# Moving the weight tiles and the x tiles of a decoder layer by 32 and 64 bytes in SBUF

## The chip, the cores and the metric

The kernel runs on one core of a Trainium2 chip. The metric is the device time of one execution in microseconds (us), as the median of several runs. The matrix engine, TensorE (PE in the profile), multiplies a stationary operand of 128x128, which a weight load (PEld) puts in place, by a moving operand of up to 512 columns. VectorE (DVE), ScalarE (ACT) and GpSimd (POOL) do the elementwise work. The queue of SyncE (SP) issues nearly all transfers from HBM. [...]

## The reference

One decoder layer on x of 512 tokens by 1024 channels, in float32: a half-step SwiGLU feed-forward block (FFN), a mixer in which a recurrent group of channels and 8 heads of stick-breaking attention stand side by side, and a second half-step FFN. Cut to what matters here:

```python
def _swiglu(x, w_gate, w_up, w_down):
    return (jax.nn.silu(x @ w_gate) * (x @ w_up)) @ w_down

x = x + 0.5 * _swiglu(_rms_norm(x, ffn1_norm), ffn1_w_gate, ffn1_w_up, ffn1_w_down)
h = _rms_norm(x, mix_norm)
xr, gate, q, k, v = split(h @ w_in)
y_rnn = _rg_lru_group(xr, gate, ...)
y_att = _stick_breaking(norm(q), norm(k), v)
x = x + concat(norm(y_rnn), norm(y_att)) @ w_out
x = x + 0.5 * _swiglu(_rms_norm(x, ffn2_norm), ffn2_w_gate, ffn2_w_up, ffn2_w_down)
```

The FFN's inner width is 2816. Nearly all of the work is the products of x with the weights.

## The kernel before

x is held transposed, channels across the 128 partitions, as eight tiles of 128x512. Each float32 operand is split into a high and a low part of the type float32r, and a product is three matmuls: high by high, high by low, low by high (`mm3`, L142 to L145). So a weight tile `r_...` that a transfer brings becomes a tile `h_...` (a cast on ACT, L133) and a tile `l_...` (a subtraction on DVE, L135), and x becomes `xh_...` and `xl_...` (L157, L159).

The work in order of time:

- The first stage (L529 to L580): 16 small matmuls on constants, then the products for the first three blocks of the first FFN. Their weights have tiles of their own, `first_r`, `first_h` and `first_l`, in a pool of their own. For each of x's eight tiles and each of the three kinds of product, six matmuls follow each other, one per weight tile, into six PSUM banks.
- The rest of the first FFN: plain products for three more blocks (L143 to L145), then sixteen blocks in pairs by a scheme that adds and subtracts halves of the matrices to save products (`fast`, L397, with moving operands of 256 columns, or 512 in some steps). Between its steps lie blocks of the down projection (L143 to L145), whose moving operands are `hh` and `hl`.
- The mixer: projections with w_in (L143 to L145; for q, k and v the weights are the moving operand and x's parts the stationary one), small gates, scores, transposes through `ident`, and w_out.
- The second FFN, as the first (tiles ending in b instead of a), without a stage of its own pool.

The order of each engine's instructions is fixed when the program is built, by a scheduler; at run time an instruction waits only for its operands and for room. The places of the tiles in SBUF are fixed then too: the pools lie one behind the other, and each tile takes the next free address, its size rounded up to 32 bytes per partition. The pool `const` comes first (`mhalf`, `warm`, `ones`, `ident`, `fut`, ...), then `wpool` (all `r_`, `h_`, `l_` tiles of weights), then `xpool` (`x0`, in which the vectors of gains and biases stand behind x's first 512 columns, x1 to x7, `xh`, `xl`), then `stat`, then the pools of the stages (`first`, then `ffn_a`, ...). A change in the size of an early tile thus moves all that lie behind it.

Of the kernel before, what the change touches and what calls it, by code (L numbers as in the profile page):

```python
# [8 lines left out]
F32 = mybir.dt.float32  # L9
# [6 lines left out]
P = 128  # L16
# [30 lines left out]
C_G1, C_GM, C_G2 = 0, 8, 16  # L47
C_CW, C_CB, C_BA, C_BX, C_LAM = 24, 40, 44, 48, 52
C_RN, C_AN, C_QN, C_KN = 56, 60, 64, 65
NVEC = 66  # L50


@with_exitstack
def hybrid_layer_kernel(
# [17 lines left out]
    const = ctx.enter_context(tc.tile_pool(name="const", bufs=1))  # L72
# [22 lines left out]

    mhalf = const.tile([P, 8], F32, tag="mhalf", name="mhalf")
    nc.vector.memset(mhalf, -0.5)
    warm = const.tile([P, 8], F32, tag="warm", name="warm")
    nc.scalar.activation(warm, mhalf, AF.Sigmoid)
    ones = const.tile([P, P], F32, tag="ones", name="ones")  # L100
# [19 lines left out]

    x0 = xpool.tile([P, T + NVEC], F32, tag="x0", name="x0")
    vec = x0[:, T:]
# [409 lines left out]
    def first_products():  # L532

        with tc.tile_pool(name="first", bufs=1, reuse_waits="tile") as fi:
# [8 lines left out]
            for kk in range(KD // 2):  # L543
                s = slice(2 * kk * P, (2 * kk + 2) * P)
                c = 2 * kk * T + NVEC
                if kk == 0:
                    nc.sync.dma_start(x0, xT[:, : T + NVEC])
                else:
# [562 lines left out]
def _layout(x, ffn1_norm, ffn1_w_gate, ffn1_w_up, ffn1_w_down, mix_norm, w_in,  # L1111
            conv_w, conv_b, rg_w_a, rg_b_a, rg_w_x, rg_b_x, rg_lambda,
            q_norm, k_norm, rnn_out_norm, attn_out_norm, w_out,
            ffn2_norm, ffn2_w_gate, ffn2_w_up, ffn2_w_down):
    import numpy as np

    def cols(v):
        return np.asarray(v).reshape(-1, P).T

    def by_block(w):  # L1120

        k, n = w.shape
        return w.reshape(k // P, P, n // P, P).transpose(2, 1, 0, 3).reshape(n // P, P, k)

    def by_pairs(w):


        o = by_block(w).reshape(NF, P, KD, P)
        o = np.concatenate([o[:, :, 0::2], o[:, :, 1::2]], axis=2).reshape(NF, P, KD * P)
        o = np.concatenate([o[1::2], o[0::2]], axis=2)  # L1130
        b = by_block(w)
        o[: PLAIN // 2] = np.concatenate([b[0:PLAIN:2], b[1:PLAIN:2]], axis=2)
        return o

    w = np.asarray(w_in)[0]
    qkv = w[:, 2 * DR :].reshape(KD // 2, 2, P, 3, DR).transpose(3, 0, 2, 1, 4)
    def gates(a, x):

        a, x = np.asarray(a)[0], np.asarray(x)[0]
        o = np.empty((P, NJ, P), a.dtype)  # L1140
        for n in range(2 * NJ):
            r = (n % 2) * HD
            o[r : r + HD, n // 2, r : r + HD] = a[n]
            o[r : r + HD, n // 2, HD - r : 2 * HD - r] = x[n]
        return o.reshape(P, NJ * P)

    def swapped(v):

        return np.asarray(v).reshape(-1, 2, HD)[:, ::-1].reshape(-1)

    vecs = np.concatenate(
        [
            cols(ffn1_norm[0]), cols(mix_norm[0]), cols(ffn2_norm[0]), cols(conv_w[0]),
            cols(conv_b[0]), cols(rg_b_a[0]), cols(swapped(rg_b_x[0])), cols(rg_lambda[0]),
            cols(rnn_out_norm[0]), cols(attn_out_norm[0]),
            cols(np.tile(np.asarray(q_norm[0]), 2)), cols(np.tile(np.asarray(k_norm[0]), 2)),
        ],
        axis=1,
    )

    xt = np.asarray(x)[0].T.reshape(KD, P, T).transpose(1, 0, 2).reshape(P, KD * T)
    a = {
        "xT": np.concatenate([xt[:, :T], vecs, xt[:, T:]], axis=1),
        "w_rg": by_block(w[:, : 2 * DR]),
        "w_qkv": qkv.reshape(3, KD // 2, P, 2 * DR),
        "w_gate": gates(rg_w_a, rg_w_x),
        "w_out": by_block(np.asarray(w_out)[0]),
        "wg1": by_pairs(np.asarray(ffn1_w_gate)[0]),
        "wu1": by_pairs(np.asarray(ffn1_w_up)[0]),
        "wd1": by_block(np.asarray(ffn1_w_down)[0]),  # L1170
        "wg2": by_pairs(np.asarray(ffn2_w_gate)[0]),
        "wu2": by_pairs(np.asarray(ffn2_w_up)[0]),
        "wd2": by_block(np.asarray(ffn2_w_down)[0]),
    }
    return {n: np.ascontiguousarray(a[n]) for n in _INS}
# [21 lines left out]
```

## Time and profile before

| | |
|---|---|
| median of 3 runs | 909.22 us (908.8 to 909.35) |
| the profiled execution | 908.92 us |
| its span, first to last instruction | 907.1 us |
| PE busy | 901.0 us, 99% of the span, 4880 matmuls |
| weight loads busy | 758.1 us, 84% |
| DVE busy | 712.9 us, 79% |
| ACT busy | 466.9 us, 51% |
| POOL busy | 72.9 us, 8% |
| moved by DMA | 89.18 MB, 29.0% of the 16 engines' time on the main queue |

The duration that the profile gives for a matmul (about 395 ns for 512 columns) includes the way through the array, and the next one starts before it is over; what a stream of matmuls costs is read from the distance between starts, here called the spacing. PE's busy share therefore also covers short gaps.

### The profile page before, as it was taken

The numbers are of one execution on the slowest core, as the hardware profiler recorded it, in microseconds if no ns is written. First come the engines' busy times: TensorE is split into PE (matmuls) and PEld (weight loads), VectorE is DVE, ScalarE is ACT, GpSimd is POOL, SyncE is SP. The second block draws the span as 40 slices with busy tenths as digits, with TensorE's granted clock in tenths as the row PEclk, the third lists the DMA queues.
The fourth block names the chain that finished last, engine by engine and source line by source line (L and its number), as shares of the span: only waits on it lengthen the run. The fifth ranks groups of instructions, "written<-read, shape, count | busy, mean of one in ns | idle before, by whom it ended". The sixth has DMA issues, their size and how long they took to land.

```text
span 907.1 us, 12596 instructions
## 1 busy us (share of the span) xinstructions
PE 901.0 (99%) x4880; PEld 758.1 (84%) x4880; DVE 712.9 (79%) x1032; ACT 466.9 (51%) x771; POOL 72.9 (8%) x60
## 2 busy tenths in 40 slices
PE   9999999999999999999999999999999999999998
PEld 7888899888988888877887678888899888998887
DVE  8598789887887669758689959697689967896763
ACT  7254365544653446365768844445256534563450
POOL 0000000000000005544140001400000000000000
PEclk9999999999999999999999999999999999999999
DMA  8323322331232222322132002324322332233202
GB/s 284 106 62 138 115 93 93 133 141 53 94 128 93 76 93 83 115 72 103 58 116 71 25 24 94 117 66 149 117 93 93 120 129 78 93 112 99 88 24 92
DMA packets 27452, 89.18 MB, mean 98 GB/s; under 512 B 2817, under 2 KB 6145, under 8 KB 23297
## 3 DMA queue, kind: packets, MB, share of 16 engines
q1 hardware_dynamic: 27248, 88.26, 29.0%
q8 instruction: 38, 0.62, 0.3%
q14 instruction: 22, 0.17, 0.1%
q10 hardware_dynamic: 144, 0.13, 0.0%
HBM read 86.28 MB, written 2.10 MB: 97 GB/s over the span
## 4 chain that ended last, share of the span: by engine, by line
PE 98%; DVE 1%; DMA 0%; issue 0%; ACT 0%; DVEq 0%
PE pxua L397 5%; PE pxub L397 5%; PE pxgb L397 5%; PE pxga L397 5%; PE pdb L144 5%; PE pdb L145 5%; PE pdb L143 5%; PE pda L144 5%; PE pda L145 5%; PE pda L143 5%; PE pyua L397 4%; PE pyga L397 4%; PE pygb L397 4%; PE pyub L397 4%; PE first_p L580 4%; PE po L143 2%
## 5 line engine op out<-in xcount | busy, mean ns | idle before, releaser
L144 PE MATMUL pdb<-hlb,h_db 128*128 128x512 f32 (+2 forms) x180 | 70.1, 391 | 0.0
L145 PE MATMUL pdb<-hhb,l_db 128*128 128x512 f32 (+2 forms) x180 | 69.7, 391 | 0.0
L143 PE MATMUL pdb<-hhb,h_db 128*128 128x512 f32 (+2 forms) x180 | 69.3, 391 | 0.0
L144 PE MATMUL pda<-hla,h_da 128*128 128x512 f32 x176 | 69.2, 395 | 0.0
L145 PE MATMUL pda<-hha,l_da 128*128 128x512 f32 x176 | 68.9, 395 | 0.0
L143 PE MATMUL pda<-hha,h_da 128*128 128x512 f32 x176 | 68.0, 395 | 0.0
L482 DVE SCALAR_TENSOR_TENSOR x<-pdb,x 128x512 f32<-128x512 f32 (+2 forms) x33 | 21.9, 673 | 35.8 <-PE pdb L145 35.8
L133 ACT CAST h_da<-r_da 128x768 fp32r<-128x768 f32 (+1 forms) x28 | 24.2, 867 | 43.5 <-PE pda L144 21.4
L133 ACT CAST h_db<-r_db 128x768 fp32r<-128x768 f32 (+1 forms) x28 | 24.2, 868 | 41.3 <-PE pdb L144 21.8
L482 DVE SCALAR_TENSOR_TENSOR x<-pda,x 128x512 f32<-128x512 f32 x32 | 21.6, 687 | 27.2 <-PE pda L145 27.2
L145 PEld LDWEIGHTS pdb<-hhb,l_db 128*128 128x128 f32 x180 | 33.8, 188 | 7.7
L144 PEld LDWEIGHTS pdb<-hlb,h_db 128*128 128x128 f32 x180 | 33.8, 188 | 7.2
L143 PEld LDWEIGHTS pdb<-hhb,h_db 128*128 128x128 f32 x180 | 33.8, 188 | 6.9
L145 PEld LDWEIGHTS pda<-hha,l_da 128*128 128x128 f32 x176 | 33.0, 187 | 7.9
L144 PEld LDWEIGHTS pda<-hla,h_da 128*128 128x128 f32 x176 | 33.0, 187 | 7.3
L143 PEld LDWEIGHTS pda<-hha,h_da 128*128 128x128 f32 x176 | 33.0, 188 | 7.1
L173 POOL TENSOR_TENSOR sqa_m<-sqa_m,sq_m 128x512 f32<-128x512 f32 x7 | 11.8, 1681 | 312.4 <-ACT sq_m L172 312.2
L377 ACT CAST h_gb<-rgb 128x512 fp32r<-128x512 f32 (+1 forms) x24 | 18.4, 765 | 24.2 <-PE pdb L144 12.8
L135 DVE TENSOR_TENSOR l_da<-r_da,h_da 128x768 fp32r<-128x768 f32 (+1 forms) x28 | 27.7, 989 | 2.9 <-ACT h_da L133 2.9
L135 DVE TENSOR_TENSOR l_db<-r_db,h_db 128x768 fp32r<-128x768 f32 (+1 forms) x28 | 27.7, 992 | 2.9 <-ACT h_db L133 2.9
L377 ACT CAST h_ua<-rua 128x512 fp32r<-128x512 f32 (+1 forms) x24 | 18.3, 764 | 22.5 <-PE pyga L397 8.8
L377 ACT CAST h_ub<-rub 128x512 fp32r<-128x512 f32 (+1 forms) x24 | 18.4, 765 | 22.1 <-PE pygb L397 8.8
(459 smaller groups left out, 2821.3 us busy)
## 6 DMA issues: line engine op xcount, KB each, us to landing
r_da<-in_wd SPq DMA_DIRECT2D x24, 384.0 KB, 3.1
r_db<-in_wd SPq DMA_DIRECT2D x24, 384.0 KB, 3.1
rga<-in_wg SPq DMA_DIRECT2D x8, 1024.0 KB, 5.7
rua<-in_wu SPq DMA_DIRECT2D x8, 1024.0 KB, 4.7
rgb<-in_wg SPq DMA_DIRECT2D x8, 1024.0 KB, 5.0
rub<-in_wu SPq DMA_DIRECT2D x8, 1024.0 KB, 4.8
r_o<-in_w_out SPq DMA_DIRECT2D x8, 512.0 KB, 3.5
r_gb<-in_wg SPq DMA_DIRECT2D x6, 512.0 KB, 3.8
```

The lines of the kernel that those rows point to most:

```text
L133: nc.scalar.copy(hi, raw)
L135: nc.vector.tensor_sub(lo, raw, f32(hi))
L143: nc.tensor.matmul(out_, wh, ah, start=start, stop=False)
L144: nc.tensor.matmul(out_, wh, al, start=False, stop=False)
L145: return nc.tensor.matmul(out_, wl, ah, start=False, stop=stop)
L173: (engine or nc.gpsimd).tensor_add(self.acc, self.acc, sq)
L377: nc.scalar.copy(hi[:, to], a)
L397: nc.tensor.matmul(pt[:, : r.shape[1]], l[:, s], r, start=start and (k, i) == order[0], stop=(k, i) == order[-1], skip_group_check=True,)
L482: nc.vector.scalar_tensor_tensor(x[k][:, t], pt[:, t], 0.5, x[k][:, t], op0=ALU.mult, op1=ALU.add)
L580: nc.tensor.matmul(pts[i], wp[i][:, s], xp[k], start=k == 0 and wp is hi and xp is n1.h, stop=k == KD - 1 and wp is lo,)
```

## The change

The change adds a tile of eight float32 columns, which nothing reads or writes, between `mhalf` and `warm` in the pool `const`, and 14 columns of zeros behind the vectors in `x0` (NVEC goes from 66 to 80; the host's array gets the same zeros).

```diff
-NVEC = 66
+NVEC = 80
...
     nc.vector.memset(mhalf, -0.5)
+    const.tile([P, 8], F32, tag="space", name="space")
     warm = const.tile([P, 8], F32, tag="warm", name="warm")
...
             cols(np.tile(np.asarray(q_norm[0]), 2)), cols(np.tile(np.asarray(k_norm[0]), 2)),
+            np.zeros((P, NVEC - C_KN - 1), np.float32),
```

What it does to the places in the built program, as the remainder of a tile's start address on division by 64, and by 128 in brackets (x0's row with vectors grows from 2312 to 2368 bytes, and the room that it takes from 2336 to 2368):

| tiles | before | after | moved by |
|---|---|---|---|
| `ones`, `ident`, `fut` and the other constants behind `warm` | 0 (64) | 32 (96) | 32 |
| weights in `wpool`: `r_`, `h_`, `l_` | 0 (64) | 32 (96) | 32 |
| `x0` | 0 (64) | 32 (96) | 32 |
| x1 to x7, `xh`, `xl` | 32 (96) | 32 (32) | 64 |
| weights of the first stage: `first_r`, `first_h`, `first_l` | 32 (96) | 32 (32) | 64 |
| FFN tiles: `hh`, `hl`, `xb`, `g`, `o`, `raw`, `sums` | 32 (96) | 32 (32) | 64 |
| mixer: `qT`, `kT`, `gate_h`, `gate_l` | 32 (96) | 32 (32) | 64 |
| mixer: `xch`, `xcl` | 0 (0) | 0 (64) | 64 |

Slices of weights start at multiples of 512 bytes inside their tile, and the moving operands of 512 columns at multiples of 2048.

No instruction is added or removed. The transfer of x0 brings 592 instead of 578 columns. The orders of DVE, ACT, POOL and SP are the same but for the numbers of the tiles. On PE one matmul of the first stage moves back. Before, the product of the last low weight tile (`first_l_138`) with x's first tile (`xh_a_172`) comes ahead of the products with x's second tile (`xh_a_188`):

```order
L580 MATMUL first_p_127<-xh_a_172,first_l_126 128x512
L580 MATMUL first_p_135<-xh_a_172,first_l_134 128x512
L580 MATMUL first_p_139<-xh_a_172,first_l_138 128x512
L580 MATMUL first_p_119<-xh_a_188,first_h_117 128x512
L580 MATMUL first_p_123<-xh_a_188,first_h_121 128x512
L580 MATMUL first_p_127<-xh_a_188,first_h_125 128x512
L580 MATMUL first_p_131<-xh_a_188,first_h_129 128x512
L580 MATMUL first_p_135<-xh_a_188,first_h_133 128x512
L580 MATMUL first_p_139<-xh_a_188,first_h_137 128x512
```

Now, with every line and tile number one higher, it stands five places later in the same stretch of PE's order:

```order
L581 MATMUL first_p_128<-xh_a_173,first_l_127 128x512
L581 MATMUL first_p_136<-xh_a_173,first_l_135 128x512
L581 MATMUL first_p_120<-xh_a_189,first_h_118 128x512
L581 MATMUL first_p_124<-xh_a_189,first_h_122 128x512
L581 MATMUL first_p_128<-xh_a_189,first_h_126 128x512
L581 MATMUL first_p_132<-xh_a_189,first_h_130 128x512
L581 MATMUL first_p_136<-xh_a_189,first_h_134 128x512
L581 MATMUL first_p_140<-xh_a_173,first_l_139 128x512
L581 MATMUL first_p_140<-xh_a_189,first_h_138 128x512
```

Only this matmul moved; the rest of PE's 4393 rows keeps its order.

## Rows read from the trace of the kernel before

**Rows 1.** The page: busy time of the engines (us, share of the span, instructions), and the chain that ended last, by engine.

```profile
PE 901.0 (99%) x4880; PEld 758.1 (84%) x4880; DVE 712.9 (79%) x1032; ACT 466.9 (51%) x771; POOL 72.9 (8%) x60
...
PE 98%; DVE 1%; DMA 0%; issue 0%; ACT 0%; DVEq 0%
```

**Rows 2.** The view of waits, PE alone: who waited for whom, us in total, times, the longest. These are all its rows.

```profile
PE warm L529 <- DVE ones L101: 1.1, 1, 1.1
PE py L1012 <- DVE yal L1027: 0.8, 1, 0.8
PE pw L993 <- DVE be L984: 0.6, 1, 0.6
PE first_p L580 <- ACT xh_a L157: 0.5, 1, 0.5
PE py L1012 <- ACT wt L1004: 0.3, 1, 0.3
```

**Rows 3.** The chain that ended last, from 105 to 114 us, in order of time: start in us, us on the chain, what. On the chain a matmul's us is its spacing.

```profile
105.13 0.23 PE pda L143
...
107.23 1.40 PE pxga L397 x8
108.64 1.40 PE pyga L397 x8
110.04 1.41 PE pxua L397 x12
111.45 1.41 PE pyua L397 x12
```

**Rows 4.** The timeline of PE in the first stage: start in us, us, what, and how many matmuls the row merges.

```profile
8.57 0.39 PE L580 MATMUL first_p<-xh_a,first_h 128*128 128x512 f32 x1
8.80 0.39 PE L580 MATMUL first_p<-xl_a,first_h 128*128 128x512 f32 x1
9.02 1.07 PE L580 MATMUL first_p<-xh_a,first_l 128*128 128x512 f32 x4
9.93 0.39 PE L580 MATMUL first_p<-xh_a,first_h 128*128 128x512 f32 x1
...
14.01 1.52 PE L580 MATMUL first_p<-xh_a,first_h 128*128 128x512 f32 x6
15.37 1.52 PE L580 MATMUL first_p<-xl_a,first_h 128*128 128x512 f32 x6
...
20.81 0.39 PE L580 MATMUL first_p<-xh_a,first_l 128*128 128x512 f32 x1
...
35.22 1.65 PE L580 MATMUL first_p<-xh_a,first_h 128*128 128x512 f32 x6
36.70 1.54 PE L580 MATMUL first_p<-xl_a,first_h 128*128 128x512 f32 x6
38.08 1.52 PE L580 MATMUL first_p<-xh_a,first_l 128*128 128x512 f32 x6
39.44 0.60 PE L200 MATMUL psr_a<-ident,r_a 128*128 128x128 f32 x4
```

**Rows 5.** Busy time by stretch: the stretch in us and its length; then busy us and instructions of PE, PEld, DVE, ACT, POOL; granted share of PE's full clock, DMA share, GB/s.

```profile
15.00:20.00 5.00, 5.00 (x24) 4.14 (x23) 5.00 (x12) 5.00 (x14) 0.00 (x0) 1.00 0.96 312
35.20:37.60 2.40, 2.40 (x12) 1.98 (x12) 0.16 (x1) 0.00 (x0) 1.02 (x1) 1.00 0.00 1
39.40:60.00 20.60, 20.60 (x92) 16.61 (x91) 20.60 (x34) 11.06 (x16) 0.00 (x0) 1.00 0.13 39
100.00:150.00 50.00, 50.00 (x335) 45.66 (x335) 41.15 (x61) 27.61 (x48) 0.00 (x0) 1.00 0.26 91
625.00:645.00 20.00, 20.00 (x88) 16.05 (x87) 17.89 (x32) 6.40 (x12) 0.00 (x0) 1.00 0.68 244
```

**Rows 6.** The same kind of view for the stretch behind the first stage, once each for the matmuls of L143, L144, L145 and L397: PE busy and its instructions, PEld busy and its instructions.

```profile
39.50:907.10 867.60, 284.92 (x724) 135.85 (x724) 1.00 0.28 93
...
39.50:907.10 867.60, 284.74 (x724) 135.86 (x724) 1.00 0.28 93
...
39.50:907.10 867.60, 283.97 (x724) 135.78 (x724) 1.00 0.28 93
...
39.50:907.10 867.60, 322.42 (x2128) 294.35 (x2128) 1.00 0.28 93
```

**Rows 7.** Groups of PE's instructions by line and shape: count, busy us, mean ns of one. Here the weights are the moving operand and a part of x the stationary one.

```profile
L144 PE MATMUL pk<-l_k,xh_m 128*128 128x512 f32 x32 | 12.7, 395 | 0.0
```

**Rows 8.** Groups of ACT's and DVE's instructions by line and shape, as in rows 7.

```profile
L377 ACT CAST h_ga<-rga 128x512 fp32r<-128x512 f32 x16 | 10.0, 622 | 9.5 <-PE pda L144 9.0 <-PE pyga L397 0.3
L271 ACT CAST hha<-gga 128x512 fp32r<-128x512 f32 x16 | 9.6, 620 | 3.8 <-DVE gga L457 1.8 <-DVE gga L456 1.4 <-PE pda L145 0.7
L378 DVE TENSOR_TENSOR l_ga<-rga,h_ga 128x512 fp32r<-128x512 f32 x16 | 10.9, 683 | 0.1
L272 DVE TENSOR_TENSOR hla<-gga,hha 128x512 fp32r<-128x512 f32 x16 | 10.5, 685 | 0.3 <-ACT hha L271 0.2
```

**Rows 9.** The timeline around 176 us, where a pair's high part becomes ready on ACT and PE takes it.

```profile
176.18 0.61 ACT L271 CAST hha<-gga 128x512 fp32r<-128x512 f32 x1
...
176.85 0.39 PE L143 MATMUL pda<-hha,h_da 128*128 128x512 f32 x1
```

## The prediction

> **What bounds the kernel now.** I read the engines' busy times and the chain first. PE is busy for 901.0 of 907.1 us, and the chain that ended last is 98% PE [rows 1]. PE's waits come to 3.3 us in all [rows 2]. So the time is the number of matmuls times their spacing, and a change that moves no work can only act on the spacing. That is what I read next, in two places.
>
> Behind the first stage the spacing of a 512-column matmul is 233 ns: from 105.13 to 107.23 us lie nine matmuls of the down projection, 2.10/9 = 233.3 ns [rows 3]. A 256-column matmul takes half of that: eight of `pxga`, four of either width, take 1.40 us, as 4 x 233.3 + 4 x 116.7 does, and twelve narrow ones take 1.40 to 1.41 us [rows 3].
>
> In the first stage it is shorter. From 14.01 to 20.81 us lie 30 matmuls of 512 columns: 6.80/30 = 226.7 ns [rows 4]. The granted clock is 1.00, the 2.4 GHz level, in both [rows 5], so the clock doesn't part them: 226.7 ns are 544 of its cycles, 32 more than there are columns, and 233.3 ns are 560, 48 more.
>
> **What differs between the two.** Not the load: from 15 to 20 us DVE and ACT are busy all the time and the DMA engines 96% of it, and the spacing is the short one [rows 4, 5]. Not the six matmuls in a row with one moving operand either: from 8.57 to 9.93 us it is xh, xl, then xh with low weights, and six matmuls take 1.36 us, 226.7 ns [rows 4]. What is left is the place of the operands. In the first stage weights and x's parts both stand at 32 modulo 64. Behind it one stands at 0 and the other at 32: weights at 0 and the moving x, `hh` or `xb` at 32, or, for q, k and v, moving weights at 0 and stationary x at 32; the matmul then lasts 395 ns like the others of the long spacing [rows 7].
>
> The short spacing is not there from the start. After the small matmuls on `sqa` at 35 us the next six take 36.70 - 35.22 = 1.48 us, of which the first takes some 0.32, so 232 ns each for five; the next six 1.38 us, 230 ns; the last six 39.44 - 38.08 = 1.36 us, 226.7 ns [rows 4]. No transfer runs then and DVE and ACT are next to idle [rows 5]. With equal places PE falls into the short spacing after some ten matmuls; with unequal places it never does.
>
> **The change part by part.**
>
> The weights go from 0 to 32 modulo 64, and x's parts and the FFN's tiles stay at 32. So all large products stand as the first stage does, modulo 64. I take the spacing to become 226.7 and 113.3 ns. Counts: L143 to L145 have 3 x 724 = 2172 matmuls, of which 24 belong to the last split block and are narrower (12 of 384, 12 of 128 columns), leaving 2148 of 512. L397 has 2128 [rows 6]. By the code an FFN has eight pairs with a g and a u matrix each; ten of these sixteen matrices (all g, and u of pairs 6 and 9) run their seven products with four matmuls of 512 and four of 256 columns, so 2 x 10 x 28 = 560 matmuls of L397 have 512 columns and 1568 have 256. Gain: (2148 + 560) x 6.6 ns = 17.9 us, and 1568 x 3.3 ns = 5.2 us: 23.1 us together.
>
> What comes off it. Each break in the stream (a transpose, a gate, an idle moment) costs the fall into the short spacing: 5 x 5.3 + 6 x 3.3 = 46 ns by the rows at 35 us [rows 4]. The mixer has some 60 such breaks (42 steps of the attention's order and some 18 gates and turns), so 2.8 us at most; many breaks are closer together than ten matmuls and then nothing is gained between them either, which the same figure covers. I take 1.5 us.
>
> PE is also fed just in time at some places. The pair at 176 us has its high part ready at 176.79 and PE takes it at 176.85 [rows 9]. If PE's fill work between a pair's last product and this point, some 8 us, shrinks by 2.8%, PE waits up to 0.23 us there. There are 16 such pairs: at most 3.7 us, and I take 2.0. From 39.4 us on DVE has no idle time for 20.6 us [rows 5], but there is no wait of PE there, and DVE is back at 82% by 100 to 150 us (41.15 of 50), 85% after a gain of 2.8%. It stays off the path.
>
> The rest costs nothing. ACT's casts take 622 ns into weights at 0 and 620 ns into `hh` at 32, DVE's subtractions 683 and 685 ns [rows 8], so the engines that write the moved tiles don't care. Transfers into weights at 32 ran at 312 GB/s with a DMA share of 0.96 in the first stage, and into weights at 0 at 244 with 0.68 [rows 5]: 325 against 359 GB/s of busy time, so a moved transfer takes 0 to 10% longer; PE waits for none of them [rows 2]. The 14 columns are 7 KB more in the first transfer, 0.02 us at 312 GB/s, ahead of the first product. The one matmul that moved in the first stage keeps the stage's work as it was, at most one spacing of 0.2 us either way.
>
> Sum: 23.1 - 1.5 - 2.0 = 19.6 us. The profiled execution took 908.9 us, so 889.3; the median of the runs is 0.3 us higher: **889.6 us**.
>
> A rule that speaks against this: the Trainium skill, "SBUF — State Buffer", section "Door 1: The DMA port swizzle", gives SBUF lines of 16 bytes, and 32 bytes are two whole lines, so by it a shift of 32 changes nothing. "TensorE: Matmul & The Clock Gate", section "Step-by-step: what each phase is for", says that loading the next weights takes no read bandwidth from the running matmul, so their relative place shouldn't count; by these rules the time stays at 909.2 us. The two spacings of 226.7 and 233.3 ns in one trace don't agree with them, unless something else parts the stages.
>
> **The rivals.**
>
> *The place isn't the cause* (chance 0.14): the first stage has six PSUM banks in turn and six weight tiles far apart, and I can't exclude that these give the short spacing; the stretch at 8.57 us, with its changing operands, speaks against it but is short. Then nothing moves: 909.2 us, 908.4 to 910.0.
>
> *Only the plain products gain* (0.14): in L397 two widths alternate every four matmuls, fewer than the ten that the fall into the short spacing took, and the trace has no 256-column matmul with equal places. Then 2148 x 6.6 ns = 14.2 us less the same 1.5 and 2.0: 10.7 us, 898.5 us.
>
> *Slower* (0.10): in the first stage weights and x's parts are equal modulo 128 too (96 and 96); after the change the large products have weights at 96 and x's parts at 32. If what counts repeats every 128 bytes and the price grows with the distance, the rows give 226.7 ns at distance 0 and 233.3 at 32, and one more such step makes 239.9 at 64: 23.1 us lost in place of 23.1 won, 932.0 us. It decides as soon as the down projection's spacing passes 233.3. For it: no row of before has the distance 64. Against it: the short spacing has 32 cycles more than columns, one for each 16 columns or 64 bytes of a moving row, which makes 64 the natural length, and by that the two places are equal.
>
> **How the numbers follow.** Forecast 0.62, the others 0.14, 0.14 and 0.10. The forecast's own range is 885 (no deduction, 886.1, less a little) to 895 us. The range that holds 8 in 10 takes in the partial gain and no change and leaves out the slower case: 885 to 910 us. Faster by over 0.2% (1.8 us, about what a measurement of this kernel can tell from none): 0.62 + 0.14 = 0.76; the same 0.14; slower 0.10.
>
> **What would show it.** Right: the nine matmuls that now span 2.10 us span 2.04, the narrow twelve 1.36 instead of 1.40, and single matmuls last 0.39 us throughout, as in the first stage [rows 4]. The first stage keeps 6.80 us for 30. Wrong in the cause: the spacing stays at 233.3. Wrong in size: the plain products at 226.7 and those of L397 at 233.3, or PE's waits grow beyond the 3.3 us of now by more than 2.0. The prediction as a whole is wrong if the spacing of the down projection doesn't fall.

## The result, and the profile after

The changed kernel takes 898.77 us in the median (898.72 to 898.83, four runs), the kernel before, measured beside it, 909.04 us (908.8 to 909.35). The ratio is 0.9888, with a 95% interval of 0.9872 to 0.9903: 10.3 us faster. The profiled execution took 898.83 us, and its span is 897.0.

The page of the changed kernel: busy times, and the chain by engine.

```profile
PE 891.2 (99%) x4880; PEld 758.0 (84%) x4880; DVE 712.1 (79%) x1032; ACT 466.2 (52%) x771; POOL 72.9 (8%) x60
...
PE 98%; DVE 1%; DMA 1%; issue 0%; ACT 0%; SPq 0%; DVEq 0%
```

PE's waits in the changed kernel: who waited for whom, us in total, times, the longest. These are all its rows.

```profile
PE warm L530 <- DVE ones L102: 1.1, 1, 1.1
PE py L1013 <- DVE yal L1028: 0.8, 1, 0.8
PE pw L994 <- DVE be L985: 0.7, 1, 0.7
PE py L1013 <- ACT wt L1005: 0.3, 1, 0.3
PE first_p L581 <- ACT first_h L565: 0.2, 1, 0.2
```

PE still bounds the kernel, with the same 98% of the chain, and its waits come to 3.1 us for 3.3 [rows 1, 2]. So the gain lies in the spacing, and the chain has it. From the changed kernel's chain, start in us, us on the chain, what:

```profile
103.11 0.23 PE pda L146
...
105.17 0.23 PE pda L146
...
106.08 1.37 PE pxga L398 x8
107.45 1.38 PE pyga L398 x8
108.84 1.41 PE pxua L398 x12
110.25 1.41 PE pyua L398 x12
```

Nine matmuls of the down projection lie between 103.11 and 105.17 us: 2.06/9 = 228.9 ns, for 233.3 before [rows 3]. The eight of `pxga` take 1.37 us for 1.40. The twelve narrow ones take 1.41 us, no less than the 1.40 to 1.41 of before. The timeline shows how 228.9 comes about:

```profile
104.78 0.39 PE L145 MATMUL pda<-hla,h_da 128*128 128x512 f32 x1
105.00 0.39 PE L146 MATMUL pda<-hha,l_da 128*128 128x512 f32 x1
105.23 0.39 PE L144 MATMUL pda<-hha,h_da 128*128 128x512 f32 x1
105.47 0.39 PE L145 MATMUL pda<-hla,h_da 128*128 128x512 f32 x1
105.69 0.39 PE L146 MATMUL pda<-hha,l_da 128*128 128x512 f32 x1
105.92 0.62 PE L398 MATMUL pxga<-xb_sa,h_ga 128*128 128x512 f32 x2
...
106.84 0.39 PE L398 MATMUL pxga<-xb_sa,l_ga 128*128 128x256 f32 x2
107.06 0.39 PE L398 MATMUL pxga<-xh_sa,l_ga 128*128 128x256 f32 x2
107.29 0.62 PE L398 MATMUL pyga<-xb_sa,h_ga 128*128 128x512 f32 x2
```

The starts repeat in threes: 0.24, 0.22, 0.23 us, in the trace's nanoseconds 232, 226 and 229. It is a third spacing, between the two of the kernel before. Behind the wide matmuls the four narrow ones from 106.84 to 107.29 take 0.45 us, 113 ns each, but in the long narrow runs the spacing is 1.41/12 = 117.5 ns. The first stage in the changed kernel, its weights and x's parts both moved by 64 bytes, keeps its 30 matmuls from 14.11 to 20.91 us, 6.80/30 = 226.7 ns, as in [rows 4]:

```profile
14.11 1.52 PE L581 MATMUL first_p<-xh_a,first_h 128*128 128x512 f32 x6
15.47 1.52 PE L581 MATMUL first_p<-xl_a,first_h 128*128 128x512 f32 x6
...
20.91 0.39 PE L581 MATMUL first_p<-xh_a,first_l 128*128 128x512 f32 x1
```

The groups of the changed kernel: line, what, count, busy us and mean ns of one. A matmul's duration here is its spacing and some 162 ns more (389 goes with 227, 392 with 230, 395 with 233), so this column can be read for the spacing:

```profile
L145 PE MATMUL pda<-hla,h_da 128*128 128x512 f32 x176 | 68.5, 391 | 0.0
...
L398 PE MATMUL pxua<-xh_sa,h_ua 128*128 128x256 f32 x72 | 13.4, 278 | 0.0
...
L145 PE MATMUL pk<-l_k,xh_m 128*128 128x512 f32 x32 | 12.7, 396 | 0.0
```

The products for q, k and v, in which the weights are the moving operand, gained nothing: `pk` lasts 396 ns, for 395 before [rows 7].

### The profile page after: what moved, and what is told of

Same layout as the page of the kernel before. It is cut to its first block, busy times and chain, and to the rows that moved or that the text cites. A ratio compares the mean times of both kernels' runs of the same rounds, so it can differ in the third digit from the quotient of the medians.

```text
span 897.0 us, 12596 instructions
## 1 busy us (share of the span) xinstructions
PE 891.2 (99%) x4880; PEld 758.0 (84%) x4880; DVE 712.1 (79%) x1032; ACT 466.2 (52%) x771; POOL 72.9 (8%) x60
## 4 chain that ended last, share of the span: by engine, by line
PE 98%; DVE 1%; DMA 1%; issue 0%; ACT 0%; SPq 0%; DVEq 0%
PE pxub L398 5%; PE pxua L398 5%; PE pxgb L398 5%; PE pxga L398 5%; PE pdb L146 5%; PE pdb L144 5%; PE pdb L145 5%; PE pda L146 5%; PE pda L144 4%; PE pda L145 4%; PE pyua L398 4%; PE pyub L398 4%; PE pyga L398 4%; PE pygb L398 4%; PE first_p L581 4%; PE po L144 2%
## 5 line engine op out<-in xcount | busy, mean ns | idle before, releaser
L145 PE MATMUL pdb<-hlb,h_db 128*128 128x512 f32 (+2 forms) x180 | 69.3, 387 | 0.0
L144 PE MATMUL pdb<-hhb,h_db 128*128 128x512 f32 (+2 forms) x180 | 68.9, 388 | 0.0
L145 PE MATMUL pda<-hla,h_da 128*128 128x512 f32 x176 | 68.5, 391 | 0.0
L144 PE MATMUL pda<-hha,h_da 128*128 128x512 f32 x176 | 67.5, 392 | 0.0
L145 PEld LDWEIGHTS pdb<-hlb,h_db 128*128 128x128 f32 x180 | 33.8, 188 | 6.5
L144 PEld LDWEIGHTS pdb<-hhb,h_db 128*128 128x128 f32 x180 | 33.8, 188 | 6.1
L145 PEld LDWEIGHTS pda<-hla,h_da 128*128 128x128 f32 x176 | 33.0, 188 | 6.6
L144 PEld LDWEIGHTS pda<-hha,h_da 128*128 128x128 f32 x176 | 33.0, 188 | 6.3
```

The costliest lines, as they stand in the source:

```text
L144: nc.tensor.matmul(out_, wh, ah, start=start, stop=False)
L145: nc.tensor.matmul(out_, wh, al, start=False, stop=False)
```

## The experiments

Every kernel of this section computes the whole layer; only empty bytes differ. The one matmul of the first stage that moved back in PE's order stands as in the changed kernel wherever columns lie behind the vectors, and as before where none do. "Distance" is the start of the moving operand less that of the stationary one, in bytes per partition of SBUF. For the large products it is 32 before and 64 after (modulo 128, and modulo 256 too); in the first stage it is 0 in both kernels; for q, k and v, where the weights move, it has the other sign. "Narrow" matmuls are those of L397 with 256 columns, its "wide" ones have 512; where lines were added ahead of it, L397 is L398, L399 or L400.

### First four: distance or place, and modulo what

The first reading of the result was theory D: the distance modulo 128 sets the spacing, and the changed kernel's 64 is a third case beside 0 and 32. Its rivals were S, by which equal places modulo 64 are all there is to win and the first stage is faster still by its structure, and P, by which each operand's own place counts.

**Both at 64 modulo 128.** Against the changed kernel:

```diff
-NVEC = 80
+NVEC = 96
...
-    const.tile([P, 8], F32, tag="space", name="space")
```

> 30 columns behind the vectors and no empty tile: weights and x's parts both start at 64 modulo 128 (both 0 modulo 64, distance 0 modulo 128). Theory D (the distance of the two places modulo 128 sets the spacing: 226.7 ns at 0, 229.0 at 64, 233.3 at 32): all large products take 226.7 and 113.3 ns, q, k and v too, 23.1 us less than before and about 1.5 lost at breaks: 887.5 us (886 to 890). Rival S (equal places modulo 64 are enough and give 229.0; the 226.7 of the first stage comes from its six weight tiles and six banks): as after, 898.8. Rival P (both have to stand at 32 modulo 64): as before, 909.

**Both at 96 modulo 128.** Against the changed kernel:

```diff
-NVEC = 80
+NVEC = 96
```

> The empty tile and 30 columns behind the vectors: weights and x's parts both start at 96 modulo 128 (both 32 modulo 64, distance 0 modulo 128). Theory D: as the run with both at 64, 887.5 us (886 to 890), 226.7 ns for 512 columns. Rival S: 898.8 with 229.0 ns. Rival P: 898.8, since both stand at 32 modulo 64 as after the change.

**Only the 14 columns**, without the empty tile:

```diff
-    const.tile([P, 8], F32, tag="space", name="space")
```

> Only the 14 columns, no empty tile: weights at 64, x's parts at 0 modulo 128 (both 0 modulo 64, distance 64 modulo 128). Theory D: as the changed kernel, 898.8 us (897.5 to 900), the plain products in the cycle of 232, 226 and 229 ns. Rival S: 898.8 too. Rival P: 909.

**Only the empty tile**, with NVEC at 66:

> Only the empty tile of eight columns, none behind the vectors: weights at 96, x's parts at 0 modulo 128 (32 and 0 modulo 64, distance 32 modulo 128). Theory D: as before, 909 us with 233.3 ns (908 to 910). Rivals S and P: 909 too. A fourth view, that any move of the tiles away from their old places helps, would give less than 905.

Measured: both at 64, 910.28 us (ratio to before 1.0018, 1.0008 to 1.0027); both at 96, 910.25; only the columns, 898.79 (0.9888, 0.9873 to 0.9902); only the tile, 908.81 (0.9999).

Two things follow. The 14 columns are the whole change: alone they give its time to 0.02 us, and the empty tile alone gives that of before. The matmul that moved in the order isn't what helps: it stands there in the kernels of 910.28 and 910.25 us too. In the pairs 898.77 and 898.79, and 910.28 and 910.25, all operands stand 32 bytes further in one kernel than in the other, and the time is the same: moving both together by 32 bytes doesn't count, the place to one another does. In the first stage, whose distance stays 0 throughout, starts at 96, 32, 64 and 0 modulo 128 (before, changed, both at 64, only the columns) all give a mean of 227 ns. But none of the theories has all four numbers. P falls with the 14 columns alone (909 expected) and with both at 96 (898.8 expected); D and S fall with both at 64 and both at 96: at distance 0 modulo 128 the kernel isn't faster, it is a little slower than before. In that kernel the first stage's matmuls last 389 ns as ever and the down projection's 395, so the two can't have what counts in common:

```profile
L144 PE MATMUL pda<-hla,h_da 128*128 128x512 f32 x176 | 69.2, 395 | 0.0
...
L580 PE MATMUL first_p<-xh_a,first_l 128*128 128x512 f32 x48 | 12.7, 389 | 0.0
```

Modulo 256 they haven't: the distance is 0 in the first stage and 128 behind it. That made the new theory, called Q: the period is 256 bytes. Its rival, S, held that the first stage is fast by its structure.

### Second four: a period of 256, and the first stage by itself

**62 columns behind the vectors**, so that the distance of the large products is 0 modulo 256. Against the kernel with both at 64:

```diff
-NVEC = 96
+NVEC = 128
```

> 62 columns behind the vectors, no empty tile: weights and x's parts both start at 64 modulo 128 as in the run with 30 columns, but their distance is 0 modulo 256 in place of 128, as it is in the first stage. Theory Q (what counts repeats every 256 bytes: 226.7 ns at 0, 233.3 at 32, 229.0 at 64, 232.4 at 128): 226.7 ns in all large products, 887.5 us (886 to 890). Rival S (the first stage's spacing comes from its six weight tiles and its order, the rest repeats every 128 bytes): as with 30 columns, 910.3.

**22 columns (NVEC 88), distance 96**, no empty tile:

> 22 columns behind the vectors, no empty tile: the distance from the weights to x's parts is 96 modulo 256. Theory Q says nothing of 96 by itself; if odd multiples of 32 are alike: 233.3 ns and 909 us (908 to 910). If it falls with the distance up to 64 and rises evenly to 128, between 229.0 and 232.4 ns: about 904.

**46 columns (NVEC 112), distance 192**, no empty tile:

> 46 columns behind the vectors, no empty tile: the distance is 192 modulo 256, which is 64 modulo 128 and 64 back from the weights modulo 256. Rival S, with a period of 128: as the changed kernel, 898.8 us (898 to 900) with the cycle of 232, 226 and 229 ns. Theory Q: another number than at 64, or the same if 64 ahead and 64 behind are alike; q, k and v, which stood at 192 after the change and kept 233 to 236 ns, speak for another: about 909.

**The first stage's weights alone, by 32 bytes.** Against the kernel before:

```diff
         with tc.tile_pool(name="first", bufs=1, reuse_waits="tile") as fi:
+            fi.tile([P, 8], F32, tag="room", name="room")
```

> The kernel before with an empty tile of 32 bytes at the head of the first stage's own pool, and nothing else: only the first stage's weights move, and stand at 128 modulo 128 for 96 before; their distance goes from 0 to 224 modulo 256. Theory Q: the first stage's 144 matmuls go from 226.7 to some 233.3 ns, 1.0 us in all (909.9 us), and six of them take 1.40 us in place of 1.36. Rival S: they stay at 226.7 ns and the time at 908.9.

Measured: distance 0, 900.67 us (0.9909, 0.9894 to 0.9924); 96, 914.25 (1.0056, 1.0041 to 1.0071); 192, 903.95 (0.9942, 0.9925 to 0.9958); the first stage's weights moved, 909.84 (1.0011, 1.0001 to 1.002).

At 96 and 192 the times lie outside what was expected (909 or 904 us; 898.8 or 909): the expectations went by the plain products and the narrow ones go their own way, as the map below shows.

The last run settles S. Nothing but the place of the first stage's weight tiles changed, and the first stage lost its short spacing. Its timeline:

```profile
14.93 1.56 PE L581 MATMUL first_p<-xh_a,first_h 128*128 128x512 f32 x6
16.33 1.56 PE L581 MATMUL first_p<-xl_a,first_h 128*128 128x512 f32 x6
17.73 1.56 PE L581 MATMUL first_p<-xh_a,first_l 128*128 128x512 f32 x6
```

Six take 1.40 us where they took 1.36 [rows 4], 233.3 ns, and the time rose by the 1.0 us that 144 x 6.7 ns make.

At distance 0 theory Q was right about the plain products of 512 columns and wrong about the kernel. Its groups:

```profile
L144 PE MATMUL pda<-hla,h_da 128*128 128x512 f32 x176 | 68.4, 390 | 0.0
...
L144 PE MATMUL pk<-l_k,xh_m 128*128 128x512 f32 x32 | 12.5, 389 | 0.0
...
L397 PE MATMUL pxua<-xh_sa,h_ua 128*128 128x256 f32 x72 | 13.7, 283 | 0.0
```

The down projection and `pk` are at 389 to 390 ns, the first stage's figure. The narrow matmuls got slower, 283 ns for 278 at distance 64: 119.2 ns in spacing where 113.3 were expected, 9.3 us over 1568 of them. That is most of what keeps the kernel from 887.5 us; the wide ones of L397, at 231.0 ns for 226.7, add 2.4 us. At distance 192 it is the other way round:

```profile
L144 PE MATMUL pda<-hla,h_da 128*128 128x512 f32 x176 | 69.3, 395 | 0.0
...
L144 PE MATMUL pk<-l_k,xh_m 128*128 128x512 f32 x32 | 12.4, 389 | 0.0
...
L397 PE MATMUL pxua<-xh_sa,h_ua 128*128 128x256 f32 x72 | 13.2, 276 | 0.0
```

The narrow ones are at their shortest, the down projection's back at 395. And `pk`, whose distance is here 256 - 192 = 64, is short. After the change it stood at 256 - 64 = 192, and this explains why q, k and v gained nothing: the sign of the distance counts. Two timelines show the narrow spacing: at distance 0 twelve matmuls go from 108.54 to 109.98 us, 1.44/12 = 120.0 ns, at distance 192 twelve from 110.28 to 111.64, 1.36/12 = 113.3 ns.

```profile
108.54 0.40 PE L397 MATMUL pxua<-xh_sa,h_ua 128*128 128x256 f32 x2
...
109.98 0.40 PE L397 MATMUL pyua<-xl_sa,h_ua 128*128 128x256 f32 x2
```

```profile
110.28 0.39 PE L397 MATMUL pxua<-xb_sa,h_ua 128*128 128x256 f32 x2
...
111.64 0.39 PE L397 MATMUL pyua<-xb_sa,h_ua 128*128 128x256 f32 x2
```

### Last four: the rest of the map, and one distance for each product

**38 columns (NVEC 104), distance 160**, no empty tile:

> 38 columns behind the vectors, no empty tile: the distance is 160 modulo 256. Theory Q with odd multiples of 32 alike for the products of 512 columns (233.3 ns at 32, 96 and 224): 233.3 ns there, so no gain from the plain products. The products of 256 columns took 116.8 ns at 32 and 120.0 at 96: by these 909 or 914 us. A number below 905 would say that odd multiples are not alike.

Measured: 913.81 us (1.005, 1.0035 to 1.0065). Of the odd multiples of 32 measured for the whole kernel none beats the kernel before, but they are not alike. The map, with the mean spacings in ns worked out from the starts of all matmuls of each profiled run (from one start to the next; those with a break in between, over 1.3 times as long, left out):

| distance modulo 256 | time, us | down projection, 512 columns (1044) | L397, 512 columns (560) | L397, 256 columns (1568) |
|---|---|---|---|---|
| 0 | 900.67 | 227.8 | 231.0 | 119.2 |
| 32 (before) | 909.04 | 233.3 | 233.2 | 116.8 |
| 64 (after) | 898.77 | 229.1 | 230.0 | 116.2 |
| 96 | 914.25 | 233.4 | 233.2 | 120.0 |
| 128 | 910.28 | 232.6 | 232.7 | 118.5 |
| 160 | 913.81 | 234.2 | 233.9 | 118.4 |
| 192 | 903.95 | 233.1 | 232.4 | 114.0 |

No distance is best for both widths; 64 is good for both. The next step was to give each kind of product its own.

**hh and hl at 0, the rest at 64.** Against the changed kernel:

```diff
         with tc.tile_pool(name=f"ffn_{name}", bufs=1, reuse_waits="tile") as fp:
+            fp.tile([P, 48], F32, tag="room", name=f"room_{name}")
...
             def operands():
+                fp.tile([P, 16], F32, tag="room_xb", name=f"room_xb_{name}")
```

> The changed kernel with 192 empty bytes ahead of the FFN's tiles and 64 ahead of xb: hh and hl come to distance 0 modulo 256 from the weights, everything else that PE multiplies keeps its 64. Theory Q, each product by its own distance: the 1044 matmuls of the down projection go from 229.1 to 227.8 ns in the mean (226.7 in their clean runs), 1.4 us: 897.4 us (897.0 to 898.0); L398 keeps 230.0 and 116.2. Rival: the distance works through the streams as a whole and not product by product: 898.8 or more.

**The same with xb at 192** (48 columns in place of 16 ahead of xb):

> As the run with hh and hl at 0 and the rest at 64, but with xb at 192. Of L398's matmuls 672 of 256 columns and 240 of 512 read xb. By the means at 64 and 192 (116.2 and 114.0; 230.0 and 232.4 ns) the first win 1.5 us and the second lose 0.6: 896.5 us (895.8 to 897.4). Rival: as products on xb and on xh follow each other in groups of six, the two distances mix and nothing is won: 897.4 or more.

Measured: 898.61 us (898.12 to 899.16; 0.9882, 0.9865 to 0.9898) and 900.12 (899.66 to 900.26; 0.9899).

In the first of the two, the down projection did what was said: 227.9 ns in the mean, 390 in its group, and PE's busy time fell from 891.2 to 890.3 us. The kernel didn't: 898.61 us is above theory Q's range and only 0.2 us below the rival's 898.8. By the starts in the profiled run the down projection won 1.2 us, but L398 (L400 here), whose distance is still 64, lost 0.7 of it: its wide matmuls went from 230.0 to 230.6 ns, its narrow ones from 116.2 to 116.4. The profiled execution didn't get shorter at all (span 897.2 us for 897.0), since the first stage's last matmul also started 0.7 us later; it waited for a cast and for xh for 1.2 us, where the changed kernel's profile has 0.2:

```profile
PE first_p L583 <- ACT first_h L567: 0.8, 1, 0.8
...
PE first_p L583 <- ACT xh_a L158: 0.4, 1, 0.4
```

Two of its four runs took 898.1 to 898.2 us and two 899.0 to 899.2, and the profiled one is of the latter. Why the wait came isn't settled, and the two shorter runs have no profile to look into.

In the second, the rival was right. The narrow matmuls on xh, whose distance is still 64, got slower as well:

```profile
L400 PE MATMUL pxua<-xh_sa,h_ua 128*128 128x256 f32 x72 | 13.6, 281 | 0.0
```

By their starts they take 118.4 ns, for 116.1 in the changed kernel, and those on xb, now at 192, take 116.6, for 114.6 where all of L397 stands at 192. Over all 1568 the mean went from 116.4 to 117.6 ns, 2.0 us. In streams that change between two distances every few matmuls (two to nine, often six), neither gets its own spacing: what a matmul takes depends on its neighbours too.

**One distance per stream: L397 at 192 throughout, the down projection at 0.** Against the kernel with 46 columns:

```diff
         with tc.tile_pool(name=f"ffn_{name}", bufs=1, reuse_waits="tile") as fp:
+            fp.tile([P, 16], F32, tag="room", name=f"room_{name}")
...
             def operands():
+                fp.tile([P, 48], F32, tag="room_xb", name=f"room_xb_{name}")
```

> 46 columns behind the vectors, no empty tile in const (the distance is 192 modulo 256, as in the run of 903.95 us), and 64 empty bytes ahead of the FFN's tiles and 192 ahead of xb: hh and hl come to 0, xb back to 192, so the down projection and the products of L397 each keep one distance throughout. Theory Q, with a stream of one distance as its unit: the down projection falls from 233.1 to 227.9 ns, 1044 x 5.2 = 5.4 us, L397 keeps 114.0 and 232.4: 898.5 us (897.8 to 899.2), within measurement of the changed kernel. Rival (neighbouring streams act on each other beyond a few matmuls): over 900.

Measured: 899.34 us (899.15 to 901.37; 0.9894, 0.9878 to 0.9911), 4.6 us less than with 46 columns alone. The down projection came to 227.6 ns, 390 in its group; the narrow ones went from 114.0 to 114.7, which costs 1.1 us. The order of PE is the same in both kernels, so the two profiles can be laid side by side matmul by matmul: all of the 1.1 us lies in the 598 narrow ones among the first 29 matmuls of L397 behind a block of the down projection, 1.8 ns each in the mean, and the other 970 lose 0.01 us together. So a change of distance is felt for more than a few matmuls behind it. The rival had the cause right and its price too high: 899.34 us is a little above the range expected by theory Q and below the rival's 900. (The profiled execution is the longest of the four, 901.37 us. In its first stage the starts lie 0.43 us apart up to 10.3 us, for 0.23 with 46 columns, and the stage's last start comes 2.0 us later; why, its profile doesn't show.) Neither this nor the kernel of 898.61 us beats the changed one by more than can be measured.

## Why the prediction was right, and where it was not

The direction and its reason held: PE bounds the kernel, no work moved, and the place of the operands sets the spacing. The kernel came out 9.2 us above the forecast of 889.6, with 10.3 us won of 19.6. It lies outside the forecast's own range, 885 to 895, and inside that of 885 to 910 only because this one was drawn wide enough for the rivals; the sum did not carry it there.

- **"All large products stand as the first stage does, modulo 64."** This is the step that failed. It took 64 bytes for the length that counts, from the 32 cycles by which the short spacing exceeds the columns. The first stage's distance is 0 and that of the large products was now 64, and by the runs these differ: what counts repeats after 128 no more than after 64, and is the same at 0 modulo 256 in the first stage and in the down projection of the kernel with 62 columns (226.7 ns in the one, 227.8 in the mean in the other). By the same step a distance of 128 would have won as much, and the two kernels that have it lost 1.3 to 1.4 us. That 64 happens to be one of the better remainders was luck as far as this step goes.
- **The sum.** The distance of 64 has its own prices. By the starts in the two traces: the 1860 plain products won 7.5 us in all, 4.1 ns each where no break follows, and 6.6 ns were put down; q, k and v, 288, won nothing; 560 wide ones of L397 won 3.2 ns, 1.8 us; 1568 narrow ones won 0.6 ns, 1.0 us, where 3.3 ns were put down. Together 10.3 us, as measured.
- **The deductions.** The 2.0 us for waits weren't needed, with half the gain: PE's waits are 3.1 us for 3.3. The 1.5 us for breaks stay untested by themselves.
- **What was costed at nothing** was nothing: DVE 712.1 us for 712.9, ACT 466.2 for 466.9 [rows 1]. The first stage with its one moved matmul ended 0.1 us later, at 39.55 us for 39.44 [rows 4].
- **What was read from [rows 4]**, that the first stage is faster by place and not by its structure, was right, and is now shown by the run that moved its weights by 32 bytes.
- **The rivals.** "The place isn't the cause" fell with that run and with the 14 columns alone. "Only the plain products gain" named nearly the time, 898.5 us, but its mechanism isn't what happened: the plain products didn't reach 226.7 ns, part of them gained nothing, and L397 gained 2.8 us. "Slower" was right that 64 isn't 0 and wrong in its price: it let the spacing grow with the distance, and it doesn't (233.3 ns at 32, 229.1 at 64, 233.4 at 96). That no row of before has the distance 64 was the doubt to follow: the rows gave no price there, and the forecast took that of distance 0.
- **The rules weighed there.** The Trainium skill, "SBUF — State Buffer", section "Door 1: The DMA port swizzle", has lines of 16 bytes; and the Trainium skill, "TensorE: Matmul & The Clock Gate", section "Step-by-step: what each phase is for", has the loading of the next weights take no read bandwidth from the running matmul. From these the prediction drew that a shift of 32 changes nothing and that the operands' relative place shouldn't count. The runs here differ by 13.6 us (900.67 and 914.25) for 160 empty bytes, with equal work and a granted clock of 1.00 in both. The measurement decides: for these float32r products the relative place counts. Whether the loading of weights has a part in it, no run here shows.

## What to carry to other kernels

Where PE is busy without gaps, compute the spacing of a few clean runs (starts over count) in every stage; here two stages of the same shape differed by 3%, and empty columns were enough to change it. Try several distances between stationary and moving tiles in steps of 32 bytes over at least 256, and look at each width by itself, since the best for 512 columns (0) is the worst but one for 256. From one stage that is fast one may learn that place matters, but not modulo what: that takes a run at each remainder.

## What the runs showed of the hardware beyond what was expected

- The spacing of float32r matmuls with a weight load each depends on the distance of moving and stationary operand, with a period above 128 bytes, and 256 fits all runs: in the kernel with 62 columns `xh` stands at 0 modulo 512 and `hh` at 256, and the plain products on them average 227.5 and 227.8 ns. At 512 columns the cleanest runs take 226.7 ns at 0, and a cycle of 232, 226, 229 at 64; at 256 columns 113.3 at 192 and 120.0 at 0.
- Mixed distances spoil each other: with `xb` at 192 and `xh` at 64, the narrow matmuls take 117.6 ns, more than at 192 (114.0) or 64 (116.2) alone. A block at distance 0 makes the narrow matmuls behind it, at 192, 1.8 ns longer in the mean, up to the 29th.
- Why the two widths have different best distances, why neighbours act on each other, and whether the distance that counts is that to a matmul's own weights or to the next one's, no run here shows.
